# Attention: products of probabilities and values for two query tiles at once, and one product per head for the compressed branch

## The chip, the cores and the metric

The kernel runs on one core of one Trainium2 chip. The metric is the device time of one execution in microseconds (us), given as the median of several runs. Five engines work in parallel, each through its own instruction queue in order: PE (TensorE, the matrix unit; its weight loads are listed apart as PEld), DVE (VectorE), ACT (ScalarE), POOL (GpSimd) and SP (SyncE, which here only issues DMAs). They wait for each other through semaphores.

## What is computed

The program is one layer: a mixer with three branches (a short convolution, a sparse attention, a gated delta rule), then a mixture of 32 experts. The change lies in the attention, which for 512 tokens and 8 heads adds three attentions with a gate each: over 31 compressed blocks, over selected blocks and over a window. With 512 tokens the selection takes all blocks and the window reaches all earlier tokens, so both are plain causal attentions over different keys and values. Cut to what matters:

```python
p_c = softmax(s_c) * any(ok_c);  o_c = einsum('bghqc,bcgd->bqghd', p_c, v_c)      # compressed
p_s = softmax(s_s);              o_s = einsum('bghqk,bgqkd->bqghd', p_s, v_sel)   # selected
p_w = softmax(s_w);              o_w = einsum('bghqk,bkgd->bqghd', p_w, v_wb)     # window
o = gate[0] * o_c + gate[1] * o_s + gate[2] * o_w
```

The heads have 64 dimensions; four heads share keys and values (group `g`).

## The kernel before

One function, `tile_hybrid_kernel`, writes the whole program; a scheduler then puts the instructions of each engine in an order of its own, by a simulated time line, and that order is fixed when the program runs. So work of neighbouring stages is mixed: while the attention (lines 786 to 834) runs, PE also does the products of a branch (lines 187 to 189, tiles `pmm` and `pb`, called filler here: 128 rows by 512 columns each, in fp32r).

The attention loops over `j`, the pair of heads 2j and 2j+1 (`hh` 0 and 1), and inside it over `qt`, the query tile of 128 tokens: 0, 1, 2, 3, and for the last `j` 3, 2, 1, 0. A query tile sees the `nk` = 128 (qt + 1) keys up to its own end, in key tiles `kt`. For one (j, qt) there are four maps of probabilities, `i` = 2 br + hh, with `br` 0 for the selected and 1 for the window branch:

- scores (lines 797, 798): two products into `pss`, one bank per head, of `nk` columns;
- DVE adds the bias and takes the maximum (800), ACT takes the exponential (807), DVE scales by gate over sum (821), all on the tile `p_`;
- transposing (825): qt + 1 products with the identity, 128 columns each, into the bank `ptp` (two banks, one per head `hh`), and ACT copies the bank to `pT` (827; two tags with two buffers each);
- the products with the values (831): the stationary operand is the value tile, 128 keys by 64 dimensions, so a product takes half of PE's columns; head 0 writes partitions 0 to 63 of the bank `po`, head 1 partitions 64 to 127. The moving operand is `pT`, 128 columns per key tile;
- the compressed branch (816) opens the sum of the query tile in `po`: 32 keys by 64 dimensions per head, 128 columns of `pcT`.

`po` is one bank for the 512 tokens of a pair of heads. When all is in it, ACT copies it to `yn` (834). After the last `j` the copy of `yn` is split for the next branch (536, 537), whose products (187 to 189) read it. Behind the attention come that branch, the output projection, routing, and the experts, whose weights (192 MB) SP loads into a ring of buffers: first behind the loads of the branch, then as buffers come free.

Of the kernel before, what the change touches and what calls it, by code (L numbers as in the profile page):

```python
# [11 lines left out]
F32 = mybir.dt.float32  # L12
# [4 lines left out]
ALU = mybir.AluOpType  # L17
# [3 lines left out]
P = 128  # L21
S = 512
D = 1024
KT = D // P
NT = S // P
# [74 lines left out]
def kernel(ctx, tc, x, w_in, w_nat, w_small, w_gate, w_branch, w_out, cmp_w1, cmp_w2,  # L100
                       w_rt, consts, params, norm, w_eg, w_eu, w_ed, out, dbg=None):
    nc = tc.nc
    V, A, T, G = nc.vector, nc.scalar, nc.tensor, nc.gpsimd
# [681 lines left out]
    for j in range(4):  # L785
        g = j // 2
        po = ps_t.tile([P, S], F32, tag="o", name="po")
        for qt in (range(NT) if j < 3 else (3, 2, 1, 0)):
            qs = slice(qt * P, (qt + 1) * P)
            nk = (qt + 1) * P  # L790
            mx = np_.tile([P, 4, 4], F32, tag="mx4", name="mx4", bufs=2)
# [11 lines left out]
            for i in range(4):  # L803
# [6 lines left out]
            V.tensor_tensor(out=mx[:, 3].rearrange("p (b h) -> p b h", b=2),  # L810
                            in0=mx[:, 3].rearrange("p (b h) -> p b h", b=2),
                            in1=gts[:, qt, 8:24].rearrange("p (b h) -> p b h", b=2)[:, :, 2 * j:2 * j + 2], op=ALU.mult)
            for hh in range(2):
                h = 2 * j + hh
                a = slice(32 * (h % 4), 32 * (h % 4) + 32)
                T.matmul(po[64 * hh:64 * hh + 64, qs], vc[a, g, :], pcT[a, qt, g, :], start=True, stop=False)
            for br in range(2):
                pT = []
                for hh in range(2):
                    i = 2 * br + hh  # L820
                    V.tensor_scalar(out=pts[i][:, :nk], in0=pts[i][:, :nk], scalar1=mx[:, 3, i:i + 1], scalar2=None,
                                    op0=ALU.mult)
                    ptp = ps_t.tile([P, S], F32, tag=f"n{hh}", name="ptp")
                    for kt in range(qt + 1):
                        T.transpose(ptp[:, kt * P:(kt + 1) * P], pts[i][:, kt * P:(kt + 1) * P], ident)  # L825
                    pT.append(np_.tile([P, S], F32, tag=f"pT{hh}", name="pT", bufs=2))
                    A.copy(out=pT[hh][:, :nk], in_=ptp[:, :nk])

                for kt in range(qt + 1):
                    for hh in range(2):  # L830
                        T.matmul(po[64 * hh:64 * hh + 64, qs],  # L831
                                 nkv[:, kt, 256 + 128 * br + 64 * g:256 + 128 * br + 64 * g + 64],
                                 pT[hh][:, kt * P:(kt + 1) * P], start=False, stop=br == 1 and kt == qt)
        A.copy(out=yn[:, j, :], in_=po)
    dump("yn", yn)

# [626 lines left out]
```

## Time and profile before

| | |
|---|---|
| median of 3 runs | 1193.91 us (1193.05 to 1196.35) |
| profiled execution, own time | 1194.44 us |
| its span, first to last instruction | 1192.70 us |
| chain that ended last, shares of the span | PE 68%, DMA 28%, DVE 2%, ACT 1%, POOL 1% |
| attention, from its first score product to its last product with values | 407.2 to 573.0 us |
| its columns, in instructions of PE | 128 scores, 160 transposings, 160 + 32 products with values, and 318 of the filler |

How it is read: a product in fp32 with 64 columns of weights shows as two MATMUL records, a product in fp32r or a transposing as one; a run of records on one tile is merged into one row with the count behind the x. The duration of a record reaches past the start of the next, since products are pipelined; what a piece costs PE is the distance from its start to the start of the next piece. Idle time of an engine stands in brackets with the engine that ended it.

### The profile page before, as it was taken

To read this page: it belongs to the slowest core of one execution; us is meant where nothing else is said; L and a number is where in the kernel's file an instruction comes from. 1 tells how busy PE (TensorE), PEld (TensorE's weight loads), DVE (VectorE), ACT (ScalarE), POOL (GpSimd) and SP (SyncE) were. 2 spreads that over 40 slices of the span, in tenths; PEclk is the share of its full clock that TensorE was granted. 3 is DMA by queue.
4 is the path that set the end of the run, shared out by engine and by line. 5 is a ranking of instruction groups with operands and counts; after the bars stand their busy time and mean duration, and the time that the engine had idled before them with its cause. 6 is when DMAs were issued, how large, how long until landed. Compare 5 with 4: busy or idle time off the path is not lost.

```text
span 1192.7 us, 15823 instructions
## 1 busy us (share of the span) xinstructions
PE 1097.3 (92%) x6135; PEld 705.9 (59%) x6136; DVE 556.0 (47%) x1258; ACT 328.9 (28%) x642; POOL 124.2 (10%) x206
## 2 busy tenths in 40 slices
PE   0899999999999999999999989988699979799895
PEld 0788798987788887767789934323234323233333
DVE  1686486587534685566344531113032313126554
ACT  1434343343323544566332410001010101011111
POOL 3100130420000000000000143000101010133000
PEclk9999999999999999999999999999899989899999
DMA  8133233322213322100487369999999999999982
GB/s 335 58 96 99 71 106 107 107 71 72 88 54 100 89 71 71 54 19 1 168 307 316 140 239 418 418 421 420 418 420 420 420 420 420 420 421 413 421 352 74
DMA packets 53183, 272.42 MB, mean 228 GB/s; under 512 B 8715, under 2 KB 12683, under 8 KB 28272
## 3 DMA queue, kind: packets, MB, share of 16 engines
q1 hardware_dynamic: 44928, 254.95, 55.1%
q0 software_dynamic: 5600, 12.09, 2.6%
q10 hardware_dynamic: 2576, 4.32, 1.0%
q8 instruction: 50, 0.82, 0.3%
q14 instruction: 29, 0.24, 0.1%
HBM read 267.25 MB, written 12.34 MB: 234 GB/s over the span
## 4 chain that ended last, share of the span: by engine, by line
PE 68%; DMA 28%; DVE 2%; ACT 1%; POOL 1%; issue 0%; SPq 0%; POOLq 0%; ACTq 0%; DVEq 0%
DMA we<-in_w_eu_dram 16%; PE pmm L189 8%; PE pmm L187 8%; PE pmm L188 8%; DMA we<-in_w_ed_dram 8%; PE pgu L1178 5%; PE pgu L1177 4%; PE po L831 3%; PE pd L1219 3%; PE ptp L825 2%; PE pb L188 2%; PE pb L187 2%; DMA we<-in_w_eg_dram 2%; PE pb L189 2%; DMA yrows<-zero 2%; PE pmn L556 1%
## 5 line engine op out<-in xcount | busy, mean ns | idle before, releaser
L1177 PE MATMUL pgu<-we,xT 128*64 128x512 f32 x512 | 239.2, 616 | 26.7 <-DMA we<-in_w_eg_dram 24.6
L1178 PE MATMUL pgu<-we,xT 128*64 128x512 f32 x512 | 236.7, 612 | 6.9 <-DMA we<-in_w_eu_dram 6.9
L189 PE MATMUL pmm<-hTh,lo 128*128 128x512 f32 x432 | 171.9, 398 | 0.2 <-DVE lo L182 0.2
L187 PE MATMUL pmm<-hTh,hi 128*128 128x512 f32 x432 | 171.1, 396 | 0.0
L188 PE MATMUL pmm<-hTl,hi 128*128 128x512 f32 x432 | 170.7, 395 | 0.0
L182 DVE TENSOR_TENSOR lo<-raw,hi 128x1024 fp32r<-128x1024 f32 x82 | 100.6, 1227 | 116.0 <-ACT hi L181 114.7
L1177 PEld LDWEIGHTS pgu<-we,xT 128*64 128x64 f32 x512 | 68.5, 141 | 113.8 <-issue 103.1
L181 ACT CAST hi<-raw 128x1024 fp32r<-128x1024 f32 x82 | 86.1, 1050 | 165.1 <-PE pmm L188 94.8
L1219 PE MATMUL pd<-we,aT 128*64 128x512 f32 x496 | 121.9, 598 | 5.6 <-DVE y L1211 4.0
L1178 PEld LDWEIGHTS pgu<-we,xT 128*64 128x64 f32 x512 | 67.9, 140 | 68.8 <-issue 54.3
L1188 ACT ACTIVATE act<-pgu,rg 64x512 f32<-64x512 f32 x32 | 21.8, 681 | 294.4 <-PE pgu L1178 192.1
L1189 DVE SCALAR_TENSOR_TENSOR act<-pgu,rg,act 64x512 f32<-64x512 f32 x32 | 24.2, 757 | 149.7 <-ACT act L1188 149.4
L189 PEld LDWEIGHTS pmm<-hTh,lo 128*128 128x128 f32 x432 | 81.5, 189 | 17.9 <-DVE lo L182 1.8
L187 PEld LDWEIGHTS pmm<-hTh,hi 128*128 128x128 f32 x432 | 81.7, 189 | 16.6 <-DVE fa L704 0.6
L188 PEld LDWEIGHTS pmm<-hTl,hi 128*128 128x128 f32 x432 | 81.6, 189 | 16.5
L1219 PEld LDWEIGHTS pd<-we,aT 128*64 128x64 f32 x496 | 35.3, 136 | 65.8 <-issue 54.0
L1276 DVE TENSOR_TENSOR x<-pc,x 128x512 f32<-128x512 f32 (+2 forms) x76 | 45.5, 656 | 41.3 <-PE pc L1274 41.0
L1196 DVE COPY aT<-pt 128x256 f32<-128x256 f32 x32 | 13.5, 423 | 71.0 <-PE pt L1195 66.8
L1274 PE MATMUL pc<-y,sel 128*128 128x512 f32 (+2 forms) x152 | 44.4, 417 | 2.3 <-DVE x L1276 1.4
L1210 ACT CAST y<-pd 64x512 fp32r<-64x512 f32 (+2 forms) x40 | 21.2, 538 | 86.9 <-PE pd L1219 41.3
L1274 PEld LDWEIGHTS pc<-y,sel 128*128 128x128 f32 x152 | 24.7, 188 | 26.2 <-issue 11.6
L187 PE MATMUL pb<-yhi,hi 128*128 128x512 f32 x96 | 37.7, 398 | 1.3 <-ACT yhi L536 1.3
(794 smaller groups left out, 1762.5 us busy)
## 6 DMA issues: line engine op xcount, KB each, us to landing
we<-in_w_eg_dram SPq DMA_DIRECT2D x64, 1024.0 KB
we<-in_w_eu_dram SPq DMA_DIRECT2D x64, 1024.0 KB
we<-in_w_ed_dram SPq DMA_DIRECT2D x62, 1024.0 KB
raw<-in_w_in_dram SPq DMA_DIRECT2D x30, 512.0 KB
raw<-in_w_gate_dram SPq DMA_DIRECT2D x24, 512.0 KB
raw<-in_w_branch_dram SPq DMA_DIRECT2D x12, 512.0 KB
yrows<-zero POOLq DMA_DIRECT2D x1, 4096.0 KB, 21.6
raw<-in_w_nat_dram SPq DMA_DIRECT2D x8, 512.0 KB
```

The costliest lines, as they stand in the source:

```text
L181: A.copy(out=hi, in_=raw)
L182: V.tensor_tensor(out=lo, in0=raw, in1=hi.bitcast(F32), op=ALU.subtract)
L187: T.matmul(ps, ahi(k), bhi(k), start=start and k == 0, stop=False)
L188: T.matmul(ps, ahi(k), blo(k), start=False, stop=False)
L189: T.matmul(ps, alo(k), bhi(k), start=False, stop=stop and k == n - 1)
L831: T.matmul(po[64 * hh:64 * hh + 64, qs], nkv[:, kt, 256 + 128 * br + 64 * g:256 + 128 * br + 64 * g + 64], pT[hh][:, kt * P:(kt + 1) * P], ...
L1177: T.matmul(pgu[0:64], xs(k), wg(k), start=k == 0, stop=k == KT - 1)
L1178: ins = T.matmul(pgu[64:128], xs(k), wu(k), start=k == 0, stop=k == KT - 1)
L1189: V.scalar_tensor_tensor(out=at, in0=qk(pgu[64:128]), scalar=gsl, in1=at, op0=ALU.mult, op1=ALU.mult)
L1219: T.matmul(pd[64 * a:64 * a + 64], aT[:, k], wd(k, a), start=k == 0, stop=k == 3)
L1274: T.matmul(pc[:, 0:n], sel[:, t * P:(t + 1) * P], y[:, cols], start=i == 0, stop=i == len(src) - 1)
L1276: V.tensor_tensor(out=xo, in0=pc[:, 0:n], in1=xo, op=ALU.add)
```

## The change

Query tiles are taken in pairs: (0, 1) and (2, 3), in the last `j` (3, 2) and (1, 0). `n` counts the query tiles, and the products with the values are issued after the second tile of a pair (n odd), for both at once.

- `pT` is now one tile per map `i` (four tags, 7 x 128 columns, one buffer each), allocated for the pair. Key tile `kt` holds the 128 columns of the even and then the 128 of the odd query tile; the last key tile, which only the odd query tile sees, holds 128. `both` is the number of key tiles that both see (1 or 3).
- ACT copies from `ptp` into that layout (new line 823: `both` blocks of 128 with a step of 256 columns), and for an odd query tile also the last key tile (new line 825), so a copy of an odd tile becomes two: 32 more copies in the program.
- The products with the values (new line 838) have 256 columns for a shared key tile and 128 for the last one. Per `j` that is 24 products, 16 of them wide, where there were 40 of 128 columns: 96 in all for 160. The columns that pass are the same.
- The compressed branch (new line 830) is one product per head and `j` with 512 columns, 8 for 32, issued after the second query tile; it opens the sum of the whole bank `po`.

Scores, exponentials, transposings and the filler stay as they are in number and size. The diff:

```diff
@@ -785,7 +785,7 @@
     for j in range(4):
         g = j // 2
         po = ps_t.tile([P, S], F32, tag="o", name="po")
-        for qt in (range(NT) if j < 3 else (3, 2, 1, 0)):
+        for n, qt in enumerate(range(NT) if j < 3 else (3, 2, 1, 0)):
             qs = slice(qt * P, (qt + 1) * P)
             nk = (qt + 1) * P
             mx = np_.tile([P, 4, 4], F32, tag="mx4", name="mx4", bufs=2)
@@ -810,27 +810,35 @@
             V.tensor_tensor(out=mx[:, 3].rearrange("p (b h) -> p b h", b=2),
                             in0=mx[:, 3].rearrange("p (b h) -> p b h", b=2),
                             in1=gts[:, qt, 8:24].rearrange("p (b h) -> p b h", b=2)[:, :, 2 * j:2 * j + 2], op=ALU.mult)
-            for hh in range(2):
-                h = 2 * j + hh
-                a = slice(32 * (h % 4), 32 * (h % 4) + 32)
-                T.matmul(po[64 * hh:64 * hh + 64, qs], vc[a, g, :], pcT[a, qt, g, :], start=True, stop=False)
-            for br in range(2):
-                pT = []
+
+            if n % 2 == 0:
+                pT = [np_.tile([P, 7 * P], F32, tag=f"pT{i}", name="pT") for i in range(4)]
+            both = qt // 2 * 2 + 1
+            for i in range(4):
+                V.tensor_scalar(out=pts[i][:, :nk], in0=pts[i][:, :nk], scalar1=mx[:, 3, i:i + 1], scalar2=None, op0=ALU.mult)
+                ptp = ps_t.tile([P, S], F32, tag=f"n{i % 2}", name="ptp")
+                for kt in range(qt + 1):
+                    T.transpose(ptp[:, kt * P:(kt + 1) * P], pts[i][:, kt * P:(kt + 1) * P], ident)
+                pair = pT[i][:, 0:2 * both * P].rearrange("p (k q) -> p k q", k=both)
+                A.copy(out=pair[:, :, qt % 2 * P:qt % 2 * P + P], in_=ptp[:, 0:both * P].rearrange("p (k q) -> p k q", k=both))
+                if qt % 2:
+                    A.copy(out=pT[i][:, 2 * both * P:2 * both * P + P], in_=ptp[:, both * P:nk])
+            if n == 1:
                 for hh in range(2):
-                    i = 2 * br + hh
-                    V.tensor_scalar(out=pts[i][:, :nk], in0=pts[i][:, :nk], scalar1=mx[:, 3, i:i + 1], scalar2=None,
-                                    op0=ALU.mult)
-                    ptp = ps_t.tile([P, S], F32, tag=f"n{hh}", name="ptp")
-                    for kt in range(qt + 1):
-                        T.transpose(ptp[:, kt * P:(kt + 1) * P], pts[i][:, kt * P:(kt + 1) * P], ident)
-                    pT.append(np_.tile([P, S], F32, tag=f"pT{hh}", name="pT", bufs=2))
-                    A.copy(out=pT[hh][:, :nk], in_=ptp[:, :nk])
-
-                for kt in range(qt + 1):
-                    for hh in range(2):
-                        T.matmul(po[64 * hh:64 * hh + 64, qs],
-                                 nkv[:, kt, 256 + 128 * br + 64 * g:256 + 128 * br + 64 * g + 64],
-                                 pT[hh][:, kt * P:(kt + 1) * P], start=False, stop=br == 1 and kt == qt)
+                    h = 2 * j + hh
+                    a = slice(32 * (h % 4), 32 * (h % 4) + 32)
+                    T.matmul(po[64 * hh:64 * hh + 64], vc[a, g, :], pcT[a, :, g, :], start=True, stop=False)
+            if n % 2:
+
+                q2 = qt // 2 * 2 * P
+                for br in range(2):
+                    for kt in range(both + 1):
+                        last = n == 3 and br == 1 and kt == both
+                        for hh in range(2):
+                            T.matmul(po[64 * hh:64 * hh + 64, (q2 if kt < both else q2 + P):q2 + 2 * P],
+                                     nkv[:, kt, 256 + 128 * br + 64 * g:256 + 128 * br + 64 * g + 64],
+                                     pT[2 * br + hh][:, 2 * kt * P:(2 * kt + 2 if kt < both else 2 * kt + 1) * P],
+                                     start=False, stop=last)
         A.copy(out=yn[:, j, :], in_=po)
     dump("yn", yn)
 
```

How the instructions stand now is the scheduler's work. On PE, in the second pair of `j` = 2 (query tile 3 of `j` = 2; `p__4364` to `p__4379` before and `p__4300` to `p__4315` now are its four maps), before:

```order
L825 MATMUL ptp<-c_ident,p__4364 128x128 x4
L825 MATMUL ptp<-c_ident,p__4369 128x128 x4
L797 MATMUL pss<-k_h,qst 128x384
L798 MATMUL pss<-k_l,qst 128x384
L831 MATMUL po<-pT,nkv 64x128
L825 MATMUL ptp<-c_ident,p__4374 128x128 x4
L797 MATMUL pss<-k_h,qst 128x384
L798 MATMUL pss<-k_l,qst 128x384
L831 MATMUL po<-pT,nkv 64x128 x7
L825 MATMUL ptp<-c_ident,p__4379 128x128 x4
L797 MATMUL pss<-k_h,qst 128x384
L798 MATMUL pss<-k_l,qst 128x384
```

and now, where the same place holds the products of query tiles 2 and 3:

```order
L821 MATMUL ptp<-c_ident,p__4300 128x128 x4
L821 MATMUL ptp<-c_ident,p__4305 128x128 x4
L838 MATMUL po<-pT,nkv 64x256
L821 MATMUL ptp<-c_ident,p__4310 128x128 x4
L838 MATMUL po<-pT,nkv 64x256 x5
L838 MATMUL po<-pT,nkv 64x128
L797 MATMUL pss<-k_h,qst 128x384
L798 MATMUL pss<-k_l,qst 128x384
L821 MATMUL ptp<-c_ident,p__4315 128x128 x4
L838 MATMUL po<-pT,nkv 64x128
L797 MATMUL pss<-k_h,qst 128x384
L798 MATMUL pss<-k_l,qst 128x384
```

The score products that stood between the second map's transposing and the first product with values have moved behind; the first product follows the transposing of two maps directly.

On PE, the end of the attention, the last two query tiles of `j` = 3 (1 and 0), before:

```order
L831 MATMUL po<-pT,nkv 64x128 x3
L825 MATMUL ptp<-c_ident,p__4616 128x128 x2
L831 MATMUL po<-pT,nkv 64x128
L825 MATMUL ptp<-c_ident,p__4666 128x128
L831 MATMUL po<-pT,nkv 64x128 x3
L816 MATMUL po<-pcT,vc 64x128 x2
L825 MATMUL ptp<-c_ident,p__4671 128x128
L831 MATMUL po<-pT,nkv 64x128
L825 MATMUL ptp<-c_ident,p__4676 128x128
L831 MATMUL po<-pT,nkv 64x128
L825 MATMUL ptp<-c_ident,p__4681 128x128
L831 MATMUL po<-pT,nkv 64x128 x2
```

and now:

```order
L821 MATMUL ptp<-c_ident,p__4526 128x128 x2
L821 MATMUL ptp<-c_ident,p__4531 128x128 x2
L821 MATMUL ptp<-c_ident,p__4536 128x128 x2
L821 MATMUL ptp<-c_ident,p__4580 128x128
L821 MATMUL ptp<-c_ident,p__4585 128x128
L821 MATMUL ptp<-c_ident,p__4590 128x128
L838 MATMUL po<-pT,nkv 64x256
L821 MATMUL ptp<-c_ident,p__4595 128x128
L838 MATMUL po<-pT,nkv 64x256
L838 MATMUL po<-pT,nkv 64x128 x2
L838 MATMUL po<-pT,nkv 64x256 x2
L838 MATMUL po<-pT,nkv 64x128 x2
```

Transposings and products no longer alternate; six maps are transposed one behind the other through the two `ptp` banks, then the products follow in two groups.

## Rows read from the trace of the kernel before

**Rows 1.** Windows: PE, PEld, DVE, ACT, POOL busy (x), PEclk, DMA share, GB/s.

```profile
407.18:573.00 165.82, 165.57 (x1040) 123.81 (x1038) 104.25 (x362) 90.25 (x232) 0.00 (x0) 1.00 0.15 45
500.00:573.00 73.00, 72.75 (x531) 50.20 (x528) 43.48 (x188) 46.93 (x136) 0.00 (x0) 1.00 0.05 15
760.00:900.00 140.00, 117.00 (x524) 42.18 (x521) 31.91 (x53) 13.50 (x22) 10.15 (x10) 0.96 1.01 420
```

**Rows 2.** Tile view of `po`: records, duration ns min/median/max, first and last start, forms.

```profile
L831 PE MATMUL po<-pT,nkv x320: 272/273/324, 452.0 to 572.7; 128*64 128x128 f32 x160
L816 PE MATMUL po<-pcT,vc x64: 267/293/319, 438.3 to 570.4; 32*64 32x128 f32 x64
```

**Rows 3.** Time line of PE at 514 us: start, us, line, tile, shape, records.

```profile
514.02 0.40 PE L797 MATMUL pss<-k_h,qst 128*128 128x512 f32 x1
514.26 0.39 PE L798 MATMUL pss<-k_l,qst 128*128 128x512 f32 x1
514.58 0.65 PE L831 MATMUL po<-pT,nkv 128*64 128x128 f32 x6
515.16 0.44 PE L825 MATMUL ptp<-c_ident,p__3963 128*128 128x128 f32 x2
515.53 0.43 PE L831 MATMUL po<-pT,nkv 128*64 128x128 f32 x2
515.89 0.55 PE L825 MATMUL ptp<-c_ident,p__4013 128*128 128x128 f32 x3
516.37 0.65 PE L831 MATMUL po<-pT,nkv 128*64 128x128 f32 x6
```

**Rows 4.** Time line of PE at 522 us: longer groups.

```profile
522.32 0.87 PE L831 MATMUL po<-pT,nkv 128*64 128x128 f32 x10
523.12 0.43 PE L816 MATMUL po<-pcT,vc 32*64 32x128 f32 x4
523.48 0.66 PE L825 MATMUL ptp<-c_ident,p__4091 128*128 128x128 f32 x4
...
524.90 0.66 PE L825 MATMUL ptp<-c_ident,p__4096 128*128 128x128 f32 x4
525.49 1.09 PE L831 MATMUL po<-pT,nkv 128*64 128x128 f32 x14
526.51 0.66 PE L825 MATMUL ptp<-c_ident,p__4101 128*128 128x128 f32 x4
```

**Rows 5.** Time line of PE at 553 us: two transposings without products between.

```profile
553.58 0.66 PE L825 MATMUL ptp<-c_ident,p__4452 128*128 128x128 f32 x4
554.07 0.60 PE L825 MATMUL ptp<-c_ident,p__4457 128*128 128x128 f32 x4
```

**Rows 6.** Time line of PE at 186 us: 64-column products of 256 columns.

```profile
186.07 1.95 PE L604 MATMUL ph<-w,xv 128*64 128x256 f32 x16
187.95 0.38 PE L554 MATMUL pmn<-hi,hTh 128*128 128x256 f32 x1
```

**Rows 7.** Time line at 567 us: transposing, and ACT's copy of it.

```profile
566.97 0.44 PE L825 MATMUL ptp<-c_ident,p__4606 128*128 128x128 f32 x2
...
567.50 0.38 ACT L827 COPY pT<-ptp 128x256 f32<-128x256 f32 x1 [0.77 <-PE ptp L825]
```

**Rows 8.** ACT's groups by shape, 500 to 574 us: busy us, mean ns, idle before.

```profile
L827 ACT COPY pT<-ptp 128x512 f32<-128x512 f32 x12 | 6.9, 583 | 3.6 <-PE ptp L825 3.6
L827 ACT COPY pT<-ptp 128x384 f32<-128x384 f32 x12 | 5.7, 477 | 6.1 <-PE ptp L825 6.1
...
L827 ACT COPY pT<-ptp 128x128 f32<-128x128 f32 x11 | 2.8, 265 | 2.8 <-PE ptp L825 2.8
...
L807 ACT ACTIVATE p__4369<-p__4369,mx 128x512 f32<-128x512 f32 x1 | 0.7, 725 | 0.0
```

**Rows 9.** Time line of PE behind the attention's last product.

```profile
574.33 0.91 PE L187 MATMUL pb<-yhi,hi 128*128 128x512 f32 x2 [1.33 <-ACT yhi L536]
```

**Rows 10.** Window of one us there, columns as in rows 1.

```profile
575.00:576.00 1.00, 1.00 (x3) 0.83 (x3) 0.23 (x1) 0.00 (x0) 0.20 (x1) 0.50 0.00 0
```

## The prediction

> **What bounds the kernel now.** I read the windows first. From 407.2 to 573.0 us, the whole attention, PE is busy for 165.57 of 165.82 us, ACT for 90.25, DVE for 104.25 [rows 1]; in the last 73 us, where little filler is left, PE 72.75, ACT 46.93. So PE sets the pace there, and the others follow it: ACT's copies of `ptp` are listed with idle time ahead that PE ended [rows 8]. Its clock is full there. Behind the attention PE waits 1.33 us for `yn` to be copied and split [rows 9], then runs the next branch, and the loads of the experts' weights start behind that branch's own loads. From some 730 us on the weights bound: the DMA engines are busy without a gap, at 420 GB/s [rows 1]. Both this stream and PE's way to it start from the attention's end, so what the attention gives back should arrive at the end in full.
>
> A busy PE is not PE at its peak, so next I read the time line of PE, from start to start [rows 3, 4]. The groups of products with values tell what they consist of. A group of 2 records takes 515.89 - 515.53 = 0.36 us, one of 4 (line 816) also 0.36 (523.48 - 523.12), of 6 0.58, of 10 0.80, of 14 1.02. So four records more cost 0.22, and 0.14 is there once per group. Four records are two products, one per head: the heads' products run side by side on the two halves of the columns, and a product alone costs the same 0.22 as a pair. The scheduler sends head 0's first product as soon as its copy is there, then a transposing, then the rest: an odd number, whose last is alone again. I call 0.22 us a slot: a group of 1, 2, 3, 5, 7 products has 1, 1, 2, 3, 4 slots.
>
> A group also costs its neighbours. A score product of 512 columns ahead of another one takes 0.24, ahead of products with values 0.32 [rows 3]. Two, three and four transposings between two groups take 0.37, 0.48, 0.59 [rows 3, 4], so 0.11 each and 0.15 once; four with a group on the front side alone take 0.49 [rows 5]. So 0.10 goes with the entry into a group and 0.05 with the way out into transposings (0.10 into scores or filler). A switch from line 816 to 831 or back has the 0.14 but neither of the others: line 816 at 523.12 follows the group at 522.32 by that group's 0.80, and itself takes 0.36 [rows 4].
>
> **The wide products.** First, the width itself. Eight products of 64 by 256 columns, in pairs, take 187.95 - 186.07 = 1.88 us [rows 6]: less 0.14 that is 0.435 for a pair, twice the slot of 128 columns, to 0.01. So no time lies in the number of records, and 256 columns cost 0.44, the 512 of line 830 0.88 per pair of heads. The Trainium skill says otherwise on one point: TensorEngine Tiling (Array Packing), Instruction Overhead, gives each matmul some 60 cycles on this chip. At 2.4 GHz that would be 25 ns a record, an estimate, and 88 products of two records fewer would give 4.4 us; the rows leave 2 ns a record at most.
>
> Slots, counted over PE's order with the rule above. Before: 36 + 16 + 2 groups of one slot, 8 of two, 8 of three, 8 of four, 126 slots or 27.7 us. Now: 27.1 us, for the lone first product and the lone last one are still there and twice as wide (a pair of tiles costs a branch 1.10 or 1.98 us as the two tiles did). Gain 0.6 us.
>
> **The groups.** This is the main term. Before, the 160 + 32 products [rows 2] stand in 78 groups (a run of one line), of which neighbours 816 and 831 join some, so that 63 runs stand alone between other work. Now 96 + 8 products stand in 36 groups, all alone.
> - 42 groups fewer at 0.145: 6.1 us.
> - 27 runs fewer, each with 0.095 for the entry and 0.05 to 0.10 for the way out (by its neighbour in the order; the mean is 0.06): 4.0 us.
>
> With the 0.6 us PE has 10.7 us less to do. The sum closes on the time before: 126 slots, 78 groups and 63 runs (48.9 us), 160 transposings (17.6), 318 filler products at 0.23 (72.3), scores (20) and some 6 us for small products make 165 of the 165.8 us.
>
> What a group costs fits the skill's TensorEngine Tiling (Array Packing), Key Properties: a change of the tiling mode, not of the tile, drains the engine. The trace agrees: 816 to 831 (32 rows to 128) pays, head 0 to head 1 does not.
>
> **What is added.** ACT copies 32 tiles more. An odd tile's copy of 512 columns (583 ns) becomes 384 and 128, 477 + 265 [rows 8], so 0.16 more each, 5 us in 166, beside 76 us in which ACT was idle. The blocks are written with a step of 1 KB, which no row shows; a bound from below is nothing, from above another copy of 128 columns (265 ns), 8 us in all, still beside. The columns of the compressed products are the same. A move of `pT` to one buffer makes a copy wait for the products of the pair before; in the order these stand ahead of the transposing that feeds it, so I cost it at nothing, and at one copy (0.5 us) per pair, 4 us, if not.
>
> What is late next are ACT's copies: the products that used to lie between the transposings filled the time of the copy. From a transposing's start to its copy's start two transposings take 0.53 us [rows 7], four then 0.75.
> - Eight transposings in a row, then the first wide product (`j` = 1 and 2, second pair): PE arrives after 4 x 0.11 x 2 + 0.15 = 1.03 us, the copy of the first map's shared blocks is there after 0.75 + 0.48 + 0.1 = 1.33. A wait of 0.3; with an exponential of 725 ns ahead on ACT [rows 8] 1.0. I take 1.5 us for both.
> - The end: six maps in a row through two banks of `ptp`. Each transposing waits for the copies of the map before the last. With 0.53 or 0.42 from a transposing to its copy and 0.27 per copy, the chain runs: copies of the first map until 1.07 us, of the second until 1.61, of the third 2.15, then 2.42, 2.84; the first product at 2.7, the last map's transposing at 3.3, and 1.5 us of products: 5.0 us, where PE has 3.5 us of work (ten transposings, 1.76 us of slots, two groups). 1.5 us.
>
> Elsewhere filler or scores lie between; there I take nothing. Waits: 3.0 us, with bounds of 0 and, at 0.25 us for each of the 32 groups that read copies, 8.
>
> **Sum.** The profiled execution took 1194.44 us, 1.74 over its span. 1194.44 - 10.7 + 3.0 = 1186.7. It lies 0.5 above the median of the runs shown, so 1186.2 beside that median; I say 1186.5. The order of some weight loads and gathers behind 700 us changes too, since the scheduler's clock has moved; as the stream has no gap there [rows 1], I cost it at 0, with 1 us to either side.
>
> **Rivals.** What a measurement of this kernel can tell from no change is some 0.3%, 3.6 us.
> - *No waits.* The filler and scores cover all copies: 1194.44 - 10.7 - 0.5 = 1183.2. For it: PE waited for ACT at no place before. Against it: the order at the end.
> - *Waits take most of it.* The order was made for another clock than the chip's; if 32 groups wait 0.25 us, 1194.44 - 10.7 + 8 - 0.5 = 1191.2, and with more it is no change. For it: in the last `j` the products of a pair follow their transposing directly. To it belongs an earlier fall of PE's clock: after the 1.33 us of idle time [rows 9] the granted clock is 0.50, its lower level of 1.2 GHz, and three filler products take a microsecond instead of 0.7 [rows 10]; gaps near the end could bring that forward over 3 us of work, 1.5 to 2 us.
> - *Only the number of records counts.* If half of the 0.055 us that a record of 128 columns takes in a group were a fixed cost, and the groups' own cost stayed, 176 records fewer would give 4.8 us: 1194.44 - 4.8 + 3.0 - 0.5 = 1192.1. Against it: 0.22 at 128 and 0.435 at 256 columns [rows 3, 6] leave no fixed part. The skill's overhead per matmul, above, is this rule.
> - *Slower: the copies become the bound.* PE goes in order, so a product waiting for `pT` holds all score products behind it, DVE and ACT get their work later, and the loop PE, ACT, PE runs once per map. The mechanism would sit in the last two `j`, without filler, and has to cost more than 10.7 + 3.6 us, 0.45 us for each of 32 groups. At 0.6 us: 1194.44 - 10.7 + 19 - 0.5 = 1202. For it: one buffer of `pT` and the doubled copies. The skill's page on tiling, PSUM Bottleneck, warns of just this, evacuation as the next bound. Against it: ACT is busy for 64% of the last 73 us [rows 1], 75% with 16 odd tiles' longer copies over 68 us.
>
> **How the numbers follow.** Forecast with waits of 1 to 6 us: 0.60. No waits: 0.10. Waits take most: 0.18. Number of records: 0.03. Slower: 0.09. The range goes from 1182 (no waits, the way out of a group at 0.10 throughout) to 1191.5 (8 us of waits); outside are the slower case, some 0.07 of the waits and 0.03 below. Faster by over 0.3% is the first two cases, 0.70; within, the next two, 0.21; slower 0.09.
>
> **What would show it.** In the profile of the changed kernel: groups of 14 records with 256 columns or the like at 0.44 per pair and 0.14 once; 36 groups; the attention from its first score product to its last product some 158 us long; PE's idle time in it some 3 us, at the end and where eight transposings stand in a row; the first weight load of the experts as much earlier as the end. It would be wrong if transposings in a row cost PE more than 0.11 each, if wide products left gaps inside a group, or if the attention ends earlier and the experts don't.

## The result, and the profile after

The changed kernel takes 1185.36 us (median, 1183.90 to 1189.09) where the kernel before took 1194.28 in the same comparison: ratio 0.9928, 95% interval 0.9900 to 0.9956, so 8.9 us or 0.7% faster. Run again later beside other kernels, it gave 1184.78 us and the same ratio, 0.9928 (0.9906 to 0.9951). The forecast was 1186.5 us, within 1182.0 to 1191.5.

First the windows of the changed kernel, columns as in [rows 1]: the whole attention, its last 67 us, and the 7 us behind it.

```profile
409.50:566.80 157.30, 155.78 (x863) 113.91 (x861) 102.45 (x362) 90.62 (x265) 0.00 (x0) 1.00 0.16 48
500.00:566.80 66.80, 65.28 (x390) 41.91 (x389) 41.50 (x180) 46.59 (x155) 0.00 (x0) 1.00 0.06 17
566.80:573.80 7.00, 5.42 (x21) 3.89 (x22) 4.61 (x8) 2.82 (x4) 0.94 (x7) 1.00 0.22 64
```

From the first score product to the copy of `yn` the attention lasts 157.3 us, where it lasted 165.6 (407.4 to 573.0; [rows 1] has the same window begun 0.2 earlier). PE is still the engine that is busy throughout, with 1.5 us idle, where it was 0.25 before. What the attention gives back is passed on: as the copy of `yn` moves from 573.0 to 566.8, the first load of the experts' weights, on SP's queue, moves from 579.80 to 573.46 us (before, and now),

```profile
579.80 0.43 SPq L1071 DMA_DIRECT2D we<-in_w_eg_dram  x1
573.46 0.42 SPq L1079 DMA_DIRECT2D we<-in_w_eg_dram  x1
```

and what follows the copy takes 620.5 us instead of 619.7. In this execution the attention began 2.1 us later than before, so the span fell only by -8.3 + 2.1 + 0.8 = -5.4, from 1192.7 to 1187.3 us; it is the slowest of its four. In a second profile of each the attention began at 408.4 (changed) and 409.3 us (before), and took 157.3 and 165.6 again. So the attention's length is good to 0.1 us; its start moves by 2 us from one execution to the next, and what follows it by up to 3.

Much of that moving is PE's granted clock, which the traces show. It is 1.00 (2.4 GHz) through the attention in every profile of this document. Ahead of it, between 39 and 49 us, it falls to 0.50 (1.2 GHz) for a while: that loses 1.7 us of PE's full speed in the profiles whose attention begins at 407.2 to 407.8, and 3.4 in those where it begins at 408.4 to 409.5; both occur with the same program. From the copy of `yn` to the first product of the experts it took 124.4 and 124.3 us in the two profiles of the kernel before, with two stretches at 0.50 in between, 123.3 in the first of the changed kernel, with one (from 676 us), and 121.7 in its second, with none.

The tile view of `po`, which answers to [rows 2]:

```profile
L838 PE MATMUL po<-pT,nkv x192: 272/379/431, 464.8 to 566.5; 128*64 128x256 f32 x128, 128*64 128x128 f32 x64
L830 PE MATMUL po<-pcT,vc x16: 587/612/638, 455.8 to 552.3; 32*64 32x512 f32 x16
```

The records fell from 384 to 208, as the diff says. They stand in 36 groups. The time line of PE shows one of the two places with eight transposings in a row, and the groups behind it (columns as in [rows 3]):

```profile
541.82 0.63 PE L821 MATMUL ptp<-c_ident,p__4300 128*128 128x128 f32 x4
542.28 0.60 PE L821 MATMUL ptp<-c_ident,p__4305 128*128 128x128 f32 x4
543.01 0.65 PE L838 MATMUL po<-pT,nkv 128*64 128x256 f32 x2
543.59 0.66 PE L821 MATMUL ptp<-c_ident,p__4310 128*128 128x128 f32 x4
544.18 1.51 PE L838 MATMUL po<-pT,nkv 128*64 128x256 f32 x12
545.62 0.44 PE L797 MATMUL pss<-k_h,qst 128*128 128x384 f32 x1
...
548.68 1.73 PE L838 MATMUL po<-pT,nkv 128*64 128x256 f32 x14
550.33 0.66 PE L821 MATMUL ptp<-c_ident,p__4386 128*128 128x128 f32 x4
...
551.84 1.07 PE L830 MATMUL po<-pcT,vc 32*64 32x512 f32 x4
552.84 0.39 PE L797 MATMUL pss<-k_h,qst 128*128 128x256 f32 x1
```

Read from start to start, as before. A lone wide product takes 543.59 - 543.01 = 0.58: a slot of 0.44 and 0.14 for the group. The group of 12 records is five wide products and a narrow one, which the rule prices at 3 x 0.44 + 0.14 = 1.46; it takes 1.44. The group of 14 (1.54 + 0.14) takes 1.65, line 830 (0.88 + 0.14) 1.00. The prices taken from [rows 3, 4, 6] hold for the new shapes. From the first transposing to the first product there are 1.19 us, where PE's own work was put at 1.03: a wait of 0.16, for which no idle entry is listed, since the record of the second transposing reaches to 542.88 and leaves only 0.13 open. The other such place, at 518 us, has 1.20.

The end of the attention, where six maps are transposed through two banks:

```profile
561.93 0.44 PE L821 MATMUL ptp<-c_ident,p__4526 128*128 128x128 f32 x2
562.21 0.38 PE L821 MATMUL ptp<-c_ident,p__4531 128*128 128x128 f32 x2
562.95 0.44 PE L821 MATMUL ptp<-c_ident,p__4536 128*128 128x128 f32 x2 [0.36 <-ACT pT L825]
563.29 0.33 PE L821 MATMUL ptp<-c_ident,p__4580 128*128 128x128 f32 x1
563.97 0.33 PE L821 MATMUL ptp<-c_ident,p__4585 128*128 128x128 f32 x1 [0.35 <-ACT pT L825]
564.14 0.33 PE L821 MATMUL ptp<-c_ident,p__4590 128*128 128x128 f32 x1
564.39 0.65 PE L838 MATMUL po<-pT,nkv 128*64 128x256 f32 x2
564.97 0.33 PE L821 MATMUL ptp<-c_ident,p__4595 128*128 128x128 f32 x1
565.23 1.51 PE L838 MATMUL po<-pT,nkv 128*64 128x256 f32 x14
```

The third and the fifth map wait for the copy of the map two before. The stretch lasts from 561.93 to 566.78, 4.85 us, of which 3.5 are PE's work at the prediction's prices.

### The profile page after: what moved, and what is told of

It reads as the page before. It is cut to its first block, busy times and chain, and to the rows that moved or that the text cites. A ratio compares the mean times of both kernels' runs of the same rounds, so it can differ in the third digit from the quotient of the medians.

```text
span 1187.3 us, 15495 instructions
## 1 busy us (share of the span) xinstructions
PE 1094.1 (92%) x5959; PEld 699.4 (59%) x5960; DVE 554.3 (47%) x1258; ACT 329.4 (28%) x674; POOL 123.3 (10%) x206
## 4 chain that ended last, share of the span: by engine, by line
PE 69%; DMA 27%; DVE 2%; ACT 1%; issue 1%; POOL 1%; SPq 0%; POOLq 0%; ACTq 0%; DVEq 0%
DMA we<-in_w_eu_dram 16%; PE pmm L189 9%; PE pmm L187 9%; PE pmm L188 8%; DMA we<-in_w_ed_dram 7%; PE pgu L1186 5%; PE pgu L1185 5%; PE pd L1227 3%; PE po L838 2%; DMA we<-in_w_eg_dram 2%; PE pb L187 2%; PE pb L188 2%; DMA yrows<-zero 2%; PE pb L189 2%; PE ptp L821 2%; PE pmn L556 1%
## 5 line engine op out<-in xcount | busy, mean ns | idle before, releaser
L1219 DVE TENSOR_TENSOR y<-pd,y 64x512 fp32r<-64x512 f32 (+2 forms) x40 | 25.3, 635 | 29.6 <-ACT y L1218 29.0
```

Of the source, the lines that this page charges most:

```text
L1219: V.tensor_tensor(out=y[lo, cols], in0=pd[hi], in1=y[hi, cols].bitcast(F32), op=ALU.subtract)
```

## The experiments

Three theories were held against each other. **G**: what a switch of PE into a group of products with values and back costs sets the time, and the width of a product doesn't. **R**: half of the 0.055 us of a record of 128 columns is fixed, so fewer records are the gain. **W**: ACT's copies of `ptp` set the pace. The kernel before had a median of 1193.80 us beside the first four experiments, 1193.74 beside the next four and 1194.00 beside the last; each ratio is to the runs beside it; it is estimated from all of them and can differ from the quotient of the medians by up to 0.001. What each gave is gathered here; "counted" is slots, groups, entries and ways out over PE's order at the prediction's prices:

| kernel | groups | counted, us | PE busy in the attention | attention | median | ratio (95%) |
|---|---|---|---|---|---|---|
| before | 78 | 48.9 | 165.35 | 165.6 | 1194.28 | |
| compressed branch alone | 66 | 47.1 | 163.78 | 164.2 | 1187.48 | 0.9941 (0.9924 to 0.9957) |
| grouped, not paired | 67 | 44.1 | 160.20 | 160.2 | 1187.74 | 0.9954 (0.9942 to 0.9967) |
| changed, second copies twice | 42 | 40.5 | 159.36 | 163.7 | 1195.41 | 1.0013 (0.9997 to 1.0029) |
| changed, second copies on DVE | 41 | 40.1 | 157.99 | 161.3 | 1190.29 | 0.9972 (0.9960 to 0.9984) |
| changed, 128 columns | 46 | 38.5 | 156.72 | 159.5 | 1188.83 | 0.9949 (0.9933 to 0.9966) |
| changed | 36 | 38.1 | 155.78 | 157.3 | 1185.36 | 0.9928 (0.9900 to 0.9956) |
| changed, four banks | 35 | 37.4 | 155.37 | 156.7 | 1188.05 | 0.9954 (0.9936 to 0.9972) |
| joined | 23 | 31.3 | 150.86 | 153.4 | 1180.96 | 0.9886 (0.9870 to 0.9903) |
| joined, four banks | 23 | 31.3 | 150.91 | 153.0 | 1183.38 | 0.9917 (0.9899 to 0.9935) |

PE's busy time falls with the count, row by row, down to the last two rows, which have the same count. It falls by 71% (second copies twice) to 107% (grouped) of what is counted: 9.6 where 10.8 is counted for the change, 14.5 where 17.6 is counted for the joined kernel. The rest is short waits behind records whose modelled ends reach over them, like the 0.16 above, or a group is a little cheaper than priced; the runs don't tell these apart.

**The changed kernel with products of 128 columns.** Each wide product is issued as two, all else stays.

```diff
-                        for hh in range(2):
-                            T.matmul(po[64 * hh:64 * hh + 64, (q2 if kt < both else q2 + P):q2 + 2 * P],
...
+                        for half in range(2 if kt < both else 1):
+                            at = q2 + (half if kt < both else 1) * P
+                            for hh in range(2):
+                                T.matmul(po[64 * hh:64 * hh + 64, at:at + P],
```

> The changed kernel with each product of 256 columns written as two of 128 (160 products of 128 columns again, the compressed branch still one product per head, the pairs of query tiles and the copies kept). Measured is the attention, from the first score product to the end of the last product with values: 165.7 us before, 157.4 us with the change. Theory G (a group's switch costs, the width does not): groups 46 for 36, slots 24.9 us for 27.1, in all 38.5 us of PE for 38.1: attention 156.5 to 159, time within 2 us of the changed kernel. Theory R (half of a record's 0.055 us is fixed): 128 records more, 3.5 us: attention 161.

The attention took 159.5 us: half a microsecond over G's range and 1.5 under R's value. The time, 1188.83 us, is 3.5 above the changed kernel's, where at most 2 were expected. Its window, what PE waited for in it, and two groups:

```profile
409.00:568.50 159.50, 156.72 (x991) 120.27 (x989) 102.68 (x362) 90.41 (x264) 0.00 (x0) 1.00 0.15 47
```

```profile
PE pss L797 <- DVE mx L800: 1.2, 3, 0.7
PE ptp L821 <- ACT pT L825: 0.7, 2, 0.4
```

```profile
547.65 1.31 PE L840 MATMUL po<-pT,nkv 128*64 128x128 f32 x20
548.89 0.66 PE L821 MATMUL ptp<-c_ident,p__4351 128*128 128x128 f32 x4
...
551.12 1.52 PE L840 MATMUL po<-pT,nkv 128*64 128x128 f32 x22
552.58 0.66 PE L821 MATMUL ptp<-c_ident,p__4434 128*128 128x128 f32 x4
```

The groups settle R directly. 22 records of 128 columns take 552.58 - 551.12 = 1.46 us; the changed kernel's group of 12 records, five wide and one narrow product, passes the same eleven blocks of 128 columns in 1.44. Ten records fewer give 0.02 us. The 2.2 us that this kernel is longer are 0.94 of PE's busy time (ten groups more, but 2.2 us of slots less, since a lone product is half as wide) and 1.3 of idle time, most of it where score products wait for DVE to empty `pss` (1.2 us, where the changed kernel has 0.4). So the width is worth something after all, not inside a group but in the order that the scheduler makes of it.

**The kernel before with products grouped, not paired.** Four `pT` tiles and the products of both branches behind all four maps of one query tile; still 160 + 32 products of 128 columns.

```diff
+            pT = []
+            for i in range(4):
...
+                pT.append(np_.tile([P, S], F32, tag=f"pT{i}", name="pT", bufs=2 if i < 2 else 1))
+                A.copy(out=pT[i][:, :nk], in_=ptp[:, :nk])
             for br in range(2):
-                pT = []
...
-                                 pT[hh][:, kt * P:(kt + 1) * P], start=False, stop=br == 1 and kt == qt)
+                                 pT[2 * br + hh][:, kt * P:(kt + 1) * P], start=False, stop=br == 1 and kt == qt)
```

> The kernel before with only the grouping changed: the products of both branches are issued after all four maps of one query tile, all still 128 columns wide, no pairs, the compressed branch as before. Records as before. Theory G: 67 groups for 78, 53 runs for 63, slots 25.5 us for 27.7: PE has 4.8 us less to do, attention 161 plus waits of 0 to 2 us. Theory R: no record less, attention 165.7 or a bit more.

160.2 us, as G says and not R, and without a wait:

```profile
407.60:567.80 160.20, 160.20 (x1039) 122.78 (x1037) 103.98 (x362) 88.23 (x232) 0.00 (x0) 1.00 0.15 47
```

PE has the same 1039 records as before and is busy for 5.15 us less; 4.8 were counted, 2.6 for 11 groups and 10 runs fewer and 2.2 for slots, since fewer products stand alone. No product became wider. So an order with fewer switches, and fewer products that stand alone, brings 5.4 us without pairs or width, two thirds of the change's 8.3.

**The kernel before with only the compressed branch changed**, one product of 512 columns per head.

```diff
+        for hh in range(2):
+            h = 2 * j + hh
+            a = slice(32 * (h % 4), 32 * (h % 4) + 32)
+            T.matmul(po[64 * hh:64 * hh + 64], vc[a, g, :], pcT[a, :, g, :], start=True, stop=False)
...
-                T.matmul(po[64 * hh:64 * hh + 64, qs], vc[a, g, :], pcT[a, qt, g, :], start=True, stop=False)
```

> The kernel before with only the compressed branch changed: one product of 512 columns per head at the head of each pair of heads. Theory G: 12 groups fewer (66 for 78), no run fewer: 1.8 us less, attention 164; the compressed part is then about a sixth of the change. Theory R: 48 records fewer, 1.3 us.

In the attention just what was expected, 164.2 us: this half of the change brings 1.4 of 8.3 us. But the time fell by 6.3 us, and 613.3 us followed the attention instead of 619.7. A second profile of this kernel, and of the kernel before:

> The kernel before with only the compressed branch changed, a second time. In its first profile the attention took 164.2 us and what follows it 613.3, where it was 617 to 621 in the other kernels. If that is the order of the experts' stage, both come again within 1 us; if it was this one execution, what follows comes out at 617 or more.

> The kernel before, a second time, to see how far a stage differs between two profiles of one program. The attention should take 165.6 us again, to 0.3 us; what follows it took 619.7 and I expect 617 to 621.

The attention came out at 164.2 and 165.6 again, what follows at 613.0 and 618.9. So it belongs to the program, as far as two profiles of each can tell. The instructions behind the attention are the same in both; the scheduler's order of them isn't. On PE, the last expert of the kernel before:

```profile
1170.64 1.47 PE L1346 MATMUL pd<-we,aT 128*64 128x192 f32 x16
1171.94 1.89 PE L1219 MATMUL pd<-we,aT 128*64 128x512 f32 x8
1176.62 1.31 PE L1346 MATMUL pd<-we,aT 128*64 128x160 f32 x16 [2.79 <-DVE y L1211]
```

and of this kernel:

```profile
1167.73 1.47 PE L1346 MATMUL pd<-we,aT 128*64 128x192 f32 x16
1170.69 1.31 PE L1346 MATMUL pd<-we,aT 128*64 128x160 f32 x16 [1.49 <-DVE y L1211]
```

From the products of 192 columns to those of 160 it is 5.98 us in the one and 2.96 in the other: four products of line 1219 (eight records, 1.89 us) had been left between them, and PE waits 1.3 us less. That is 3.0 of the 6.4 us. Another 2.9 are there already when the products of 192 columns start, 597.6 us behind the attention's end in the one and 594.7 in the other, and 0.5 come later.

Of these 2.9, 2.7 are there at the first product of the experts, 124.4 us behind the copy of `yn` in the one and 121.7 in the other (in the second profiles 124.3 and 121.7). Here PE's granted clock differs (two windows of the kernel before, then the same two of this one):

```profile
573.00:583.00 10.00, 8.68 (x30) 6.35 (x31) 5.10 (x8) 2.94 (x4) 2.66 (x8) 0.83 0.42 125
683.00:693.00 10.00, 8.21 (x24) 3.82 (x25) 7.90 (x59) 2.08 (x4) 1.08 (x8) 0.83 0.79 310
573.00:583.00 10.00, 8.36 (x35) 6.32 (x35) 5.10 (x8) 3.82 (x5) 2.39 (x8) 1.00 0.42 126
683.00:693.00 10.00, 8.02 (x25) 3.31 (x24) 8.92 (x60) 2.29 (x4) 2.18 (x6) 1.00 0.65 260
```

A mean clock of 0.83 over 10 us is 1.7 us of PE's full speed lost, 3.4 in the two windows, which are the only ones with a fall between the attention and the experts. The compressed branch alone has neither fall in either profile. So nearly half of what it gained behind the attention goes with the clock; why the clock stayed up is open, since PE's idle time ahead of the first of these windows is 1.33 us in both.

The stream of weights ends earlier too: from 1153 to 1163 us, 580 to 590 behind the attention's end in both, the kernel before still moves 297 GB/s, this one 152 (first the kernel before):

```profile
1153.00:1163.00 10.00, 9.65 (x42) 3.73 (x38) 5.00 (x9) 0.68 (x1) 0.00 (x0) 1.00 0.76 297
1153.00:1163.00 10.00, 10.00 (x50) 4.14 (x48) 7.05 (x20) 0.00 (x0) 0.00 (x0) 1.00 0.44 152
```

How much of that is the earlier start and how much an order of its own was not followed.

**Joined**: the changed kernel, with the products of a pair issued behind the last transposing of the pair.

```diff
-                    T.transpose(ptp[:, kt * P:(kt + 1) * P], pts[i][:, kt * P:(kt + 1) * P], ident)
+                    last_t = T.transpose(ptp[:, kt * P:(kt + 1) * P], pts[i][:, kt * P:(kt + 1) * P], ident)
...
-                for br in range(2):
+                with tc.issue_after(last_t.ins):
+                    for br in range(2):
```

> The changed kernel with the products of a pair issued after the last transposing of the pair, so that the lone first product joins its group. Theory G: 23 groups for 36, slots 24.2 us for 27.1: PE has 6.8 us less to do; up to twelve transposings now stand in a row through two banks, waits 2 to 4 us more: attention 152.5 to 155, time 3 to 5 us below the changed kernel. Rival W (the copies are the bound now, what PE saves it waits): attention 157 or more.

> The changed kernel with the products of a pair behind its last transposing, a second time: the attention 153.4 us again, to 0.3 us, what follows it 617 to 620.

153.3 us in both profiles (the window below is cut to tenths), and 1180.96 us in all, faster than both kernels. 13 groups are gone. PE is idle for 2.5 us instead of 1.5, 1.8 of it for the copies:

```profile
407.50:560.90 153.40, 150.86 (x863) 113.61 (x861) 102.83 (x362) 91.23 (x265) 0.00 (x0) 1.00 0.16 49
```

```profile
PE ptp L821 <- ACT pT L825: 1.3, 4, 0.4
PE ptp L821 <- ACT pT L823: 0.5, 2, 0.3
```

Here a pair's products wait for all its transposings, the hardest case for W; the waits cost a microsecond more, the switches gave back five.

**Four banks of `ptp` in the last query tile**, to take the wait at the end away, on the changed kernel and on the joined one; and the changed kernel again beside them.

```diff
-                ptp = ps_t.tile([P, S], F32, tag=f"n{i % 2}", name="ptp")
+                ptp = ps_t.tile([P, S], F32, tag=("n0", "n1", "s0", "s1")[i] if j == 3 and n == 3 else f"n{i % 2}", name="ptp")
```

> The changed kernel once more, for a second profile: the attention took 157.3 us in the first one, the rest behind it (copy of the last yn to the end) 620.5 us, where the kernel before took 619.7. If the attention's length belongs to the program, it is 157.0 to 157.6 again; what the rest varies by between two executions of one program is then a bound for what the profiles can tell of it.

> The changed kernel with four banks instead of two for the four transposed maps of the very last query tile (the score banks, free by then). If the waits at the end are what the prediction made of them (1.5 us, of which the last tile's four maps hold about half), the attention gets 0.7 us shorter by the waits and another 0.7 by one group and one lone wide product less: 155.9 to 156.6 us. If the wait is for ACT itself and not for a bank, only the second half: 156.6 to 157.0.

> The kernel with joined products (attention 153.4 us) with the four banks for the last query tile. PE's work is the same; only the waits of the last four transposings can go: attention 152.7 to 153.2 us if banks hold them, 153.4 if ACT does.

The end got shorter: from the first of the two-column-block transposings (559.59) to the copy of `yn` (563.9) it is 4.3 us instead of 4.85, with one wait of 0.35 left. From the first score product to the copy of `yn` the attention lost 0.6 us on the changed kernel (157.3 to 156.7) and 0.3 on the joined one (153.3 to 153.1). The first is less than expected and lies in the range named for a wait on ACT: 0.4 of it is PE's busy time, only 0.2 idle time, so the banks gave back 0.2 of the 0.7 us of waits. The second lies in the range named for the banks. So the banks hold PE for 0.2 to 0.3 us at the end; the rest of its wait there stayed with four.

The time didn't follow: 1188.05 against 1184.78 for the changed kernel, 1183.38 against 1180.96 for the joined one. For the changed kernel no loss of the program is shown. Its own eight executions took 1183.28 to 1184.98 us where the mean granted clock was 0.980 or 0.981, and 1186.26 to 1189.09 where it was 0.975 to 0.977; with four banks it was 1184.33 at 0.981 and 1187.66 to 1188.95 at 0.977 and 0.978, the same at like clocks. For the joined kernel the executions don't overlap (1179.35 to 1182.08, and 1182.53 to 1185.23); in the profiles 618.5 and 618.6 us follow the attention, and 1.6 us of the difference lie ahead of it, where the attention begins at 407.6 and 409.2, a difference that executions of one program show too. Whether the joined kernel lost anything by the banks themselves is open.

**The added copies on DVE**, and **each of them twice on ACT**.

```diff
-                    A.copy(out=pT[i][:, 2 * both * P:2 * both * P + P], in_=ptp[:, both * P:nk])
+                    V.tensor_copy(pT[i][:, 2 * both * P:2 * both * P + P], ptp[:, both * P:nk])
```

> The changed kernel with the 32 added copies (last key tile of an odd query tile) on DVE instead of ACT. The order changes with it: 41 groups for 36, 2.0 us more for PE by the groups. If the added copies cost nothing, as predicted: attention 158.5 to 160. If they hold PE through ACT, it is 157.3 or less.

```diff
                     A.copy(out=pT[i][:, 2 * both * P:2 * both * P + P], in_=ptp[:, both * P:nk])
+                    A.copy(out=pT[i][:, 2 * both * P:2 * both * P + P], in_=ptp[:, both * P:nk])
```

> The changed kernel with each of its 32 added copies issued twice, so 32 more copies of 128 columns on ScalarE, at 265 ns 8.5 us of work more in the attention. If those copies are hidden, as forecast, the attention stays at 157 us, plus at most 1 us for the four copies that lie in the last query tile (at 0.27 us each), and the time within 1184 to 1188 us. If the copies set the pace (theory W), the attention grows by most of 8.5 us, to 163 or more, and the time to 1190 or more.

Both are slower than the changed kernel's 1184.78, by 5.5 and 10.6 us, 4.0 and 6.4 of it in the attention. With the copies on DVE the attention's 161.2 us lie above both values expected. Their windows, with what PE waited for in the second:

```profile
408.70:570.00 161.30, 157.99 (x863) 113.98 (x861) 109.87 (x394) 85.68 (x233) 0.00 (x0) 1.00 0.14 46
```

```profile
407.50:571.20 163.70, 159.36 (x863) 113.89 (x861) 104.06 (x362) 97.13 (x297) 0.00 (x0) 1.00 0.14 46
```

```profile
PE pss L797 <- DVE mx L800: 1.3, 3, 0.7
PE ptp L821 <- ACT pT L823: 0.9, 2, 0.6
PE ptp L821 <- ACT pT L826: 0.8, 1, 0.8
...
PE po L839 <- ACT pT L823: 0.3, 1, 0.3
```

ACT is idle for 67 of 164 us in the second, yet its 32 further copies cost 6.4 us. Their records sum to 8.6 us but overlap, and ACT's busy time grows by 6.5 (90.62 to 97.13), so nearly all of it comes back. It is W's value, 163 or more, that came, against the forecast that the copies are hidden. But ACT is far from busy throughout, and the rows put it down to two things: PE's idle time grows by 2.8 us (the waits for the copies in the list sum to 2.0, those for `pss` to 1.3), and PE is busy for 3.6 us longer with the same records, for it is in 42 groups instead of 36 (2.4 us counted). So a later copy costs twice, by the wait and by the order that the scheduler makes around it; which of the groups split for which copy was not traced. On DVE the copies did likewise: 7.4 us of work more there, 41 groups, and idle time of PE up from 1.5 to 3.3 us. The Trainium skill advises to use ScalarE and VectorE both for copies out of PSUM (TensorEngine Tiling (Array Packing), PSUM Bottleneck); here moving these 32 copies to DVE lost 5.5 us, with an order of 41 groups. What the change's own 32 copies cost against none at all was not measured.

## Why the prediction was right

- **What bounds.** PE, as read from [rows 1]: in the ten kernels it is busy for 97% of the attention or more. That a shorter attention arrives at the end in full holds to 1.1 us for five of the nine kernels that differ from the one before, the changed kernel among them (8.3 in the attention, 8.9 in all). The compressed branch alone gained 5.0 us more than its attention, the second copies issued twice and the two kernels with four banks 2.2 to 3.4 less.
- **The wide products.** Their price was right to 0.03 us a group, and the width itself brings nothing on PE: 22 records take 1.46 us, 12 for the same columns 1.44. The rival of the number of records falls with that, and with the grouped kernel, which gains 5.4 us with no record fewer. The Trainium skill's overhead of some 60 cycles a matmul (TensorEngine Tiling (Array Packing), Instruction Overhead) is not in these rows.
- **The groups.** The main term, 10.1 of 10.7 us by 42 groups and 27 runs fewer, is the right mechanism: grouped alone, joined and the compressed branch alone moved the attention by -5.4, -12.2 and -1.4 us, against -4.8, -15.3 (17.6 less 2.3 of idle time more) and -1.8 counted. For the change PE's busy time fell by 9.6 for 10.8. So the sizes come out 10 to 20% too large where many groups go, if none of the difference is short waits. (The sum's 4.0 us for 27 runs is 4.2 at the prices that it names, which makes the 10.8 of the table; 318 x 0.23 in its check is 73.1, not 72.3.)
- **The waits.** 3.0 us forecast, 157.3 - (165.6 - 10.7) = 2.4 found; that is what is left over, while PE's listed idle time is 1.5. By place: the end 4.85 - 3.5 = 1.35, forecast 1.5; eight transposings in a row 0.16 + 0.17, forecast 1.5, so that term was mis-sized: the first copy was there 0.1 to 0.2 us after PE, not 0.3 to 1.0, and no exponential on ACT held it up. The remaining 0.7 lies where nothing was taken, two waits of 0.17 for `mx` among it, or is the cheaper group. Errors of both signs made the sum good.
- **The added copies.** Costed at nothing outside the end, because ACT was idle for 76 us. The step by 1 KB indeed costs nothing (the 384-column copy takes 477 ns with it, as in [rows 8]), and the attention came out at 157.3 for a forecast of 158. But the reason was wrong: the same number of copies once more costs 6.4 us. Idle time of ACT was no cover where a transposing, its copy and a product follow each other. That the change's own copies found room was not to be read from the share; in this the forecast was lucky.
- **The clock.** The fear of an earlier fall didn't come true; the runs show the opposite. Behind the attention the granted clock fell to 0.50 in both profiles of the kernel before ([rows 10] is the first) and stayed at 1.00 for at least 10 us behind it in all profiles of the nine others, although PE is idle for the same 1.32 or 1.33 us ahead of that place. So this idle time by itself doesn't bring the fall, as the rival took it to; what does is open. The sum doesn't have the 1.7 us of full speed that a fall costs.
- **What follows the attention.** Costed at 0 with 1 us to either side. For the change that was right (617.2 and 620.5 us after, 619.7 and 618.9 before, the means 0.5 apart), but by luck in part: the two profiles of one program lie 3.3 apart, and up to the experts the changed kernel is 1.0 and 2.7 us quicker than the kernel before, with fewer falls of the clock, of which the means at the end show 0.5. As a rule the bound was too narrow: the compressed branch alone moved it by 6 us.

## What to carry to other kernels

Where two kinds of matmul alternate on PE, count the switches before the products: here a group of 64-column products among 128-column ones cost 0.14 us itself and 0.15 to 0.20 for its neighbours, more than its first pair of 128 columns, while a product twice as wide cost twice as much, to 0.01 us. Whether the part on the neighbours is the switch or a short wait is not separated. Holding the products back until they can run as one group was worth more than making them wide. And an engine's idle share doesn't say what another instruction on it costs if its output is waited for: double the instruction and see.

## What had not been expected

An edit of one stage can move the end by more than the stage: 32 products made 8 moved it by 6.3 us, 1.4 of them in the stage edited, 3.0 by the order of the last expert and 2.7 where the clock differed. So the granted clock belongs to the comparison of two profiles, stretch by stretch. And 32 small copies more, 6.5 us of busy time on an engine that is idle for 40% of the stage, took 6.4 us back in the attention and 10.6 in all, the whole gain.
